# Attention and S5 output products issued in longer stretches, and a planner with new cost figures

## The chip, the cores and the metric

The kernel runs on one core of one Trainium2 chip. The metric is the device time of one execution in microseconds (us); several executions are timed and their median counts. One more execution is recorded by the hardware profiler, and all rows below are from it.

## The reference, cut to what matters

Two layers of a causal decoder trunk over 1024 tokens of width 1024, float32. Each layer is a mixer and a convolutional FFN, each followed by a residual and a LayerNorm. The mixer has an attention branch (6 heads of 64), an RG-LRU branch and an S5 state-space branch. The two places that the change touches are these products:

```python
out = jnp.einsum('bnchqk,bnkchd->bnqchd', probs, vb)          # attention: probabilities times values
...
y = (jnp.einsum('bsgp,gcp->bsgc', x_re, c_re.astype(f32))     # S5: outputs from the states,
     - jnp.einsum('bsgp,gcp->bsgc', x_im, c_im.astype(f32))   # and from the inputs within a block
     + d.astype(f32) * uf)
```

The kernel computes attention over the three dilations as one masked softmax, and S5 over blocks of 8 tokens: an output is a product of a table TK with the block's own inputs plus a product of a table CA with the states before the block.

## The kernel before

The dense projections and the FFN run as three float32r products each (high times high, high times low, low times high), 128x128 by 128x512. The FFN uses a seven-product scheme (tiles `uP` up, `dP` down). Attention's transposes and its products with the values, and all of S5, are plain float32; each such matmul shows as two matmul records in the trace.

Nothing is issued where the code states it. Engine calls are first only noted down (`Traced`), as a list of (function, arguments). `Graph` works out from tiles and regions which call needs which, and `estimate` gives each call a time; `HANDOVER` gives the delay until another engine sees a result. `sweep` and `improve` are a list scheduler that goes backward and forward over this graph with the numbers of buffers as limits (8 PSUM banks, 46 slots of 128x1024, 8 half slots of 128x512), and `make_plan` repeats it with the order that the framework makes of it (five cycles) and keeps the plan that its own model finds shortest. `issue` then issues the calls in the plan's order. All instructions therefore carry one line, L149, and are told apart by tile names.

Attention (`attend`) goes by pairs of heads p (3 per layer). For each pair there are four steps Q of 256 query rows with n = 2Q+2 key blocks of 128. `score` makes the scores (`s`), the softmax on VectorE and ScalarE (`P`). `apply(Q)` then, for each key block j, transposes the probabilities of both heads on TensorE into a bank (`pt`), copies them to a half slot (`PT`, on VectorE and ScalarE by turns), and multiplies with the values (`pv`): one matmul per head, both over 128 key rows, the first head into output partitions 0 to 63 of the bank `o`, the second into 64 to 127. So each uses one half of the array's columns. The product for block j is noted right after the copy for block j+1, and each matmul is a call of its own for the planner. In the last block of each Q only 128 query columns are computed. `fill` puts dense projections of the next pair of heads between.

S5's `outputs` makes, for each half h of the 8 group pairs, four group pairs q and two row blocks b: one TK matmul (128 rows by 128 columns, over 128 inputs) and two CA matmuls (a = real, imaginary; each over the 64 states in partitions b*64 to b*64+63, so one half of the array's rows). All go to one bank per b (`yps`). S5's `states` makes products into `vps` with column halves by turns.

The planner's figures before, for the operations concerned:

```python
HANDOVER = {"PE": 230, "DVE": 90, "ACT": 120, "POOL": 100, "SP": 0}
...
VECTOR = {"tensor_tensor": (145, 1.044), "scalar_tensor_tensor": (205, 1.05), "tensor_scalar": (180, 0.53),
```

Of the kernel before, what the change touches and what calls it, by code (L numbers as in the profile page):

```python
# [9 lines left out]
F32 = mybir.dt.float32  # L10
# [30 lines left out]
RESP = 1  # L41
HOOKS = ((0, 1, "outputs_in"), (0, 7, "glu"))
# [75 lines left out]

class NoSlot(Exception):
# [3 lines left out]
class Planner:  # L123
# [21 lines left out]
    def issue(self, tc):  # L145
        last = {}
        for n in self.order:
            f, args, kwargs = self.calls[n]
            i = f(*args, **kwargs)  # L149
            i = getattr(i, "ins", i)  # L150
            self.position[i.name] = n
            if f.__name__ == "matmul":
                bank = args[0].tensor.name
                if kwargs.get("start") and bank in last:
                    tc.add_manual_dep(i, last[bank], mybir.DependencyInfo(mybir.DependencyClass.NoSync,
                                                                          mybir.DependencyReason.DATA),
                                      reason="a bank's groups one after the other")
                last[bank] = i.name

    def scheduled(self, tc):  # L160
        return [self.position[i.name] for block in tc.compile_state.ordered_instructions_by_block.values()
                for i in block if i.name in self.position]

    def place(self, order):
        use = {}
        for t, c in enumerate(order):
            _, args, kwargs = self.calls[c]
            for a in (*args, *kwargs.values()):
                n = self.tile_of(a)
                if n is not None:  # L170
                    use[n] = (use.get(n, (t,))[0], t)
        plan, held = {}, {}
        for n, (first, last) in sorted(use.items(), key=lambda x: x[1]):
# [8 lines left out]

BANK_ALL = (1 << 4096) - 1
ENGINES = {"PE": "PE", "DVE": "DVE", "Activation": "ACT", "Pool": "POOL", "SP": "SP"}
HANDOVER = {"PE": 230, "DVE": 90, "ACT": 120, "POOL": 100, "SP": 0}
DMA_BYTES, DMA_DELAY = 380, 2000
VECTOR = {"tensor_tensor": (145, 1.044), "scalar_tensor_tensor": (205, 1.05), "tensor_scalar": (180, 0.53),
          "tensor_tensor_scan": (130, 2.1), "tensor_tensor_reduce": (250, 0.85)}
# [6 lines left out]
class Graph:  # L195
# [7 lines left out]
    def __init__(self, planner):  # L203
# [7 lines left out]
        for c, (f, args, kwargs) in enumerate(calls):  # L211
            self.engine.append(ENGINES[str(f.__self__.engine).split(".")[-1]])
# [61 lines left out]
    def estimate(self, c, name, outs, ins):  # L274
        e = self.engine[c]
        n = size(outs[0].ap[1:])
        if e == "PE":
            if name == "transpose":
                t = n / 1.2 + 2
            elif ins[0].dtype == F32R:  # L280
                t = (n + 34) / 2.4
            elif outs[0].shape[0] == 64 and n > 127:
                t = n * 1.55 / 2.4
            else:
                t = (2 * n + 8) / 2.4
        elif e == "SP":
            t, self.bytes[c] = 60, size(outs[0].ap) * 4
        else:
            n = max([n] + [size(a.ap[1:]) for a in ins])
            if e == "ACT":  # L290
                t = 205 + 0.83 * n + (150 if n == 1024 and outs[0].dtype == F32 else 0)
            elif e == "POOL":
                t = 200 + n
            elif name == "scalar_tensor_tensor" and len(outs[0].ap) > 2 and n == 1024:
                t = 2125
            else:
                a, b = VECTOR.get(name, (145, 1.044))
                t = a + b * n
        self.time[c] = round(t)
# [137 lines left out]
class Traced:  # L437
# [5 lines left out]
    def __getattr__(self, name):  # L443
        f = getattr(self.engine, name)
        return lambda *args, **kwargs: self.calls.append((f, args, kwargs))

# [53 lines left out]
def emit(tc, A, out, planner, trace):  # L500
    nc = tc.nc
    V, ACT, POOL, PE, SP = (Traced(e, planner.calls) for e in (nc.vector, nc.scalar, nc.gpsimd, nc.tensor, nc.sync))
    with ExitStack() as ctx:
# [397 lines left out]
        class S5:  # L901
# [29 lines left out]
            def states(self):  # L931
# [3 lines left out]
                for h in range(2):  # L935
                    hv = slice(h * 512, h * 512 + 512)
                    vps = [bank(f"vps{l}{a}{h}") for a in range(2)]
                    for a in range(2):
                        for q in range(4):
                            gp = h * 4 + q  # L940
                            for g2 in range(2):
                                PE.matmul(vps[a][g2 * 64:(g2 + 1) * 64, q * 128:(q + 1) * 128],
                                          lhsT=T["WvT"][a][:, gp * 128 + g2 * 64:gp * 128 + g2 * 64 + 64],
                                          rhs=U[g2][:, gp * 128:gp * 128 + 128], start=True, stop=True)
# [15 lines left out]
            def outputs(self):  # L960
# [3 lines left out]
                for h in range(2):  # L964
                    yps = [bank(f"yps{l}{b}{h}") for b in range(2)]
                    for q in range(4):
                        gp = h * 4 + q
                        c, d = slice(gp * 128, gp * 128 + 128), slice(q * 128, q * 128 + 128)
                        for b in range(2):
                            PE.matmul(yps[b][:, d], lhsT=T["TK"][b][:, c], rhs=U[b][:, c], start=True, stop=False)  # L970
                        for a in range(2):
                            for b in range(2):
                                p = slice(b * 64, b * 64 + 64)
                                PE.matmul(yps[b][:, d][:, 1:], lhsT=T["CA"][a][p, c], rhs=self.x[a][p, c][:, :127],
                                          start=False, stop=a == 1)
# [188 lines left out]
        def attend(l, p, qq, kk, vt, fill, hooks):  # L1164
# [29 lines left out]
            def apply(Q):  # L1194
                o = bank(f"o{l}{p}{Q}")
                n = 2 * Q + 2
                prev = None

                def pv(j, PT):
                    lo = 1 if j == n - 1 else 0  # L1200
                    for h in range(2):
                        PE.matmul(o[h * 64:h * 64 + 64, lo * 128:256],
                                  lhsT=vt[:, j * 128 + h * 64:j * 128 + h * 64 + 64],
                                  rhs=PT[:, h * 256 + lo * 128:h * 256 + 256], start=j == 0, stop=j == n - 1)

                for j in range(n):
# [12 lines left out]
                    if prev:  # L1219
                        pv(*prev)  # L1220
                    prev = (j, PT)
                    yield
                pv(*prev)
# [594 lines left out]
```

## Time and profile before

| what | value |
| --- | --- |
| executions timed | 2301.6, 2303.13 and 5909.03 us; median 2303.13 us |
| profiled execution, its own time | 2303.53 us |
| its span, first to last instruction | 2301.7 us |
| TensorE (PE) busy | 2242.8 us, 97% |
| weight loads (PEld) busy | 1811.4 us, 79% |
| VectorE (DVE) busy | 2045.1 us, 89% |
| ScalarE (ACT) busy | 1154.0 us, 50% |

An engine counts as busy while an instruction of its own runs; instructions overlap at their ends, so the distance from start to start tells what one costs in a dense row, and the duration tells when its result is there. In the timeline, equal instructions in a row are merged: "x4" is four records.

### The profile page before, as it was taken

Reading aid. Unit: us, or ns where it says so; the run is one execution under the profiler, and the core shown is the slowest. Engines: PE = TensorE matmul, PEld = TensorE weight load, DVE = VectorE, ACT = ScalarE, POOL = GpSimd, SP = SyncE. Lnnn points to the kernel's source line nnn. Section 1 sums busy time; section 2 is a strip of 40 time slices with the busy share of each in tenths; the row PEclk is TensorE's granted clock in tenths of the full one; section 3 lists DMA queues with packets and bytes.
Section 4 is the critical chain, followed back from the end, with each engine's and each line's share of the span. In section 5 each row is a group of like instructions: output and inputs, shape, how many; then the busy total and the mean of one; then the engine's idle time right before and its main releaser. Section 6 shows DMA issues by size and latency. Waiting matters only on the chain.

```text
span 2301.7 us, 28256 instructions
## 1 busy us (share of the span) xinstructions
PE 2242.8 (97%) x10520; PEld 1811.4 (79%) x10520; DVE 2045.1 (89%) x3357; ACT 1154.0 (50%) x1773; POOL 4.0 (0%) x8
## 2 busy tenths in 40 slices
PE   8999999999999999999998899999999999999996
PEld 6867778878888888888886677788888888788884
DVE  8888878898888989999995877888899899899999
ACT  4275673754444445444735457727455444454441
POOL 0000000000000000000000000000000000000000
PEclk9999999999999999999999899999999999999998
DMA  5321150222233435322333521401222244363312
GB/s 208 87 80 44 33 174 29 83 83 83 92 110 138 158 108 201 110 99 103 128 101 94 180 74 42 147 36 75 91 84 99 92 155 156 108 215 111 120 69 83
DMA packets 82169, 246.38 MB, mean 107 GB/s; under 512 B 12464, under 2 KB 20784, under 8 KB 82032
## 3 DMA queue, kind: packets, MB, share of 16 engines
q1 hardware_dynamic: 82032, 244.59, 31.4%
q8 instruction: 82, 1.34, 0.2%
q14 instruction: 55, 0.45, 0.1%
HBM read 176.26 MB, written 60.82 MB: 103 GB/s over the span
## 4 chain that ended last, share of the span: by engine, by line
PE 84%; DVE 10%; ACT 3%; DMA 2%; issue 1%; DVEq 0%; ACTq 0%; SPq 0%
PE uP_n L149 34%; PE dP_n L149 17%; PE o_n L149 3%; PE s_n L149 2%; PE pt_n L149 2%; DVE yf_n L149 1%; PE yps_n L149 1%; DVE cg_n L149 1%; DMA wu_n<-in_w_up_dram 1%; DVE daP_n L149 1%; PE ups00c_n L149 1%; DVE dbP_n L149 1%; PE gtps01c_n L149 1%; PE vps_01c_n L149 1%; DVE cv_n L149 1%
## 5 line engine op out<-in xcount | busy, mean ns | idle before, releaser
L149 PE MATMUL dP_n<-dbP_n,daP_n 128*128 128x512 f32 x2016 | 462.2, 391 | 12.6 <-DVE yf_n L149 11.8
L149 PEld LDWEIGHTS dP_n<-dbP_n,daP_n 128*128 128x128 f32 x2016 | 379.6, 189 | 92.5 <-issue 12.5
L149 ACT ACTIVATE dbP_n<-wr_n 128x512 fp32r<-128x512 f32 x168 | 102.8, 627 | 104.7 <-DVE wr_n L149 49.7
L149 ACT ACTIVATE wA_n<-wu_n 128x512 fp32r<-128x512 f32 x144 | 89.9, 628 | 122.4 <-PE uP_n L149 41.9
L149 ACT ACTIVATE wS_n<-wu_n 128x512 fp32r<-128x512 f32 x144 | 90.2, 630 | 111.5 <-DVE wu_n L149 41.3
L149 ACT ACTIVATE daP_n<-gr_n 128x512 fp32r<-128x512 f32 x144 | 89.5, 628 | 112.8 <-PE dP_n L149 48.2
L149 DVE SCALAR_TENSOR_TENSOR cg_n<-ga_n,small,cg_n 128x1023 f32<-128x1023 f32 x96 | 122.9, 1280 | 23.4 <-ACT cg_n L149 22.6
L149 DVE SCALAR_TENSOR_TENSOR cv_n<-va_n,small,cv_n 128x1023 f32<-128x1023 f32 x96 | 122.8, 1280 | 16.2 <-ACT cv_n L149 16.0
L149 DVE TENSOR_TENSOR yf_n<-yf_n,dP_n 128x512 f32<-128x512 f32 x192 | 127.9, 689 | 4.4 <-PE dP_n L149 2.4
L149 DVE TENSOR_TENSOR dbP_n<-wr_n,dbP_n 128x512 fp32r<-128x512 f32 x168 | 116.0, 694 | 0.3 <-ACT dbP_n L149 0.3
L149 DVE TENSOR_TENSOR daP_n<-gr_n,daP_n 128x512 fp32r<-128x512 f32 x144 | 99.8, 694 | 2.4 <-ACT daP_n L149 2.4
L149 DVE TENSOR_TENSOR wS_n<-wu_n,wS_n 128x512 fp32r<-128x512 f32 x144 | 98.2, 687 | 3.3 <-ACT wS_n L149 2.8
L149 DVE TENSOR_TENSOR wA_n<-wu_n,wA_n 128x512 fp32r<-128x512 f32 x144 | 97.8, 687 | 3.1 <-ACT wA_n L149 2.9
L149 ACT ACTIVATE cg_n<-ga_n,small 128x1024 f32<-128x1024 f32 x48 | 59.7, 1243 | 73.9 <-DVE ga_n L149 51.2
L149 PE MATMUL pt_n<-ident,P_n 128*128 128x128 f32 x432 | 74.3, 285 | 11.2 <-DVE P_n L149 10.1
L149 PEld LDWEIGHTS pt_n<-ident,P_n 128*128 128x128 f32 x432 | 53.4, 144 | 33.7 <-DVE P_n L149 11.6
L149 DVE CUSTOM_DVE_ANT_0 P_n<-s_n,mask_n 128x512 f32<-128x512 f32 (+3 forms) x96 | 55.4, 586 | 22.6 <-PE s_n L149 21.9
L149 ACT ACTIVATE cv_n<-va_n,small 128x1024 f32<-128x1024 f32 x48 | 59.4, 1238 | 24.7 <-DVE va_n L149 18.5
L149 PE MATMUL o_n<-PT_n,vt_n 128*64 128x256 f32 (+1 forms) x480 | 71.1, 375 | 0.0
L149 DVE TENSOR_TENSOR uu_n<-uP_n,p_n 128x512 f32<-128x512 f32 x96 | 65.9, 687 | 3.7 <-PE uP_n L149 3.4
L149 PE MATMUL uP_n<-T1T4h_n,wA_n 128*128 128x512 f32 x192 | 64.0, 394 | 2.1 <-DVE uu_n L149 2.1
L149 PE MATMUL uP_n<-T0T3h_n,wS_n 128*128 128x512 f32 x192 | 63.4, 391 | 2.3 <-DVE uu_n L149 2.3
(2279 smaller groups left out, 5974.7 us busy)
## 6 DMA issues: line engine op xcount, KB each, us to landing
wu_n<-in_w_up_dram SPq DMA_DIRECT2D x96, 512.0 KB, 3.5
gd<-cg_n SPq DMA_DIRECT2D x48, 512.0 KB, 2.9
gr_n<-gd SPq DMA_DIRECT2D x48, 512.0 KB, 4.4
wr_n<-in_w_down_dram SPq DMA_DIRECT2D x48, 512.0 KB, 5.1
yr_n<-hres SPq DMA_DIRECT2D x24, 512.0 KB, 3.8
hres<-yr_n SPq DMA_DIRECT2D x24, 512.0 KB, 3.2
hres<-y_n SPq DMA_DIRECT2D x16, 512.0 KB, 2.6
yf_n<-hres SPq DMA_DIRECT2D x16, 512.0 KB, 5.2
```

What stands on the lines that cost most here:

```text
L149: i = f(*args, **kwargs)
```

## The change

Three things. First, a list of calls can be bound into one `Row`, which the planner places as a single call and `issue` issues one after the other. The products with the values are bound in rows of the key blocks named in `RUNS`: for Q = 0 both blocks, for Q = 1 all four, for Q = 2 three and three, for Q = 3 four and four; a row is noted after the copy of its last block. S5's `states` products are bound in rows of one a and half. Second, in S5's `outputs` the TK matmuls are split in two column halves (m) and the order is changed: one row with all TK matmuls of a half h, then one row with all its CA matmuls, b changing with each. Third, the figures of `estimate` are new, with 350 ns (`TURN`) added for each row.

```diff
+RUNS = ((2,), (4,), (3, 6), (4, 8))
...
+TURN = 350
...
-HANDOVER = {"PE": 230, "DVE": 90, "ACT": 120, "POOL": 100, "SP": 0}
-DMA_BYTES, DMA_DELAY = 380, 2000
-VECTOR = {"tensor_tensor": (145, 1.044), "scalar_tensor_tensor": (205, 1.05), "tensor_scalar": (180, 0.53),
-          "tensor_tensor_scan": (130, 2.1), "tensor_tensor_reduce": (250, 0.85)}
+HANDOVER = {"PE": 215, "DVE": 125, "ACT": 150, "POOL": 100, "SP": 0}
+DMA_BYTES, DMA_DELAY = 370, 2050
+VECTOR = {"scalar_tensor_tensor": (127, 1.044), "tensor_scalar": (95, 0.55), "tensor_tensor_scan": (47, 2.1),
+          "tensor_tensor_reduce": (165, 1.0)}
+OTHER = 66, 1.044
...
             elif ins[0].dtype == F32R:
                 t = (n + 34) / 2.4
-            elif outs[0].shape[0] == 64 and n > 127:
-                t = n * 1.55 / 2.4
+            elif n == 1:
+                t = 109
             else:
-                t = (2 * n + 8) / 2.4
+                t = n * (8 if outs[0].shape[0] == ins[0].shape[0] == 128 else 4 if outs[0].shape[0] == 32 else 2) / 2.4
...
-                t = 205 + 0.83 * n + (150 if n == 1024 and outs[0].dtype == F32 else 0)
+                t = 75 + 0.87 * n + 115 * (len(outs) > 1) + 150 * (n == 1024 and outs[0].dtype == F32) + 140 * (n == 256)
...
+    @contextmanager
+    def row(self):
+        n = len(self.calls)
+        yield
+        self.calls[n:] = [(Row(self.calls[n:]), (), {})]
...
-                    for q in range(4):
-                        gp = h * 4 + q
-                        c, d = slice(gp * 128, gp * 128 + 128), slice(q * 128, q * 128 + 128)
-                        for b in range(2):
-                            PE.matmul(yps[b][:, d], lhsT=T["TK"][b][:, c], rhs=U[b][:, c], start=True, stop=False)
-                        for a in range(2):
+                    at = [(slice(q * 128, q * 128 + 128), slice((h * 4 + q) * 128, (h * 4 + q) * 128 + 128))
+                          for q in range(4)]
+                    with PE.row():
+                        for d, c in at:
                             for b in range(2):
-                                p = slice(b * 64, b * 64 + 64)
-                                PE.matmul(yps[b][:, d][:, 1:], lhsT=T["CA"][a][p, c], rhs=self.x[a][p, c][:, :127],
-                                          start=False, stop=a == 1)
+                                for m in (slice(0, 64), slice(64, 128)):
+                                    PE.matmul(yps[b][m, d], lhsT=T["TK"][b][:, c][:, m], rhs=U[b][:, c],
+                                              start=d.start == 0, stop=False, skip_group_check=True)
+                    with PE.row():
+                        for d, c in at:
+                            for a in range(2):
+                                for b in range(2):
+                                    p = slice(b * 64, b * 64 + 64)
+                                    PE.matmul(yps[b][:, d][:, 1:], lhsT=T["CA"][a][p, c], rhs=self.x[a][p, c][:, :127],
+                                              start=False, stop=a == 1, skip_group_check=True)
...
+                def pv():
+                    with PE.row():
+                        for j, PT in ready:
+                            lo = 1 if j == n - 1 else 0
+                            for h in range(2):
+                                PE.matmul(o[h * 64:h * 64 + 64, lo * 128:256],
+                                          lhsT=vt[:, j * 128 + h * 64:j * 128 + h * 64 + 64],
+                                          rhs=PT[:, h * 256 + lo * 128:h * 256 + 256], start=j == 0, stop=j == n - 1)
+                    ready.clear()
...
-                    if prev:
-                        pv(*prev)
-                    prev = (j, PT)
+                    ready.append((j, PT))
+                    if j + 1 in RUNS[Q]:
+                        pv()
                     yield
-                pv(*prev)
```

## Rows read from the trace of the kernel before

**Rows 1.** The page: busy time by engine, and the chain that ended last by engine.

```profile
PE 2242.8 (97%) x10520; PEld 1811.4 (79%) x10520; DVE 2045.1 (89%) x3357; ACT 1154.0 (50%) x1773; POOL 4.0 (0%) x8
...
PE 84%; DVE 10%; ACT 3%; DMA 2%; issue 1%; DVEq 0%; ACTq 0%; SPq 0%
```

**Rows 2.** Windows: stretch, length, busy us by engine, granted clock, DMA share, GB/s.

```profile
82.00:110.00 28.00, 28.00 (x149) 21.84 (x148) 22.09 (x25) 9.14 (x12) 0.00 (x0) 1.00 0.28 81
1197.00:1243.00 46.00, 46.00 (x226) 37.12 (x225) 18.95 (x17) 14.40 (x18) 0.00 (x0) 1.00 0.34 87
1243.00:1294.00 51.00, 37.16 (x164) 28.15 (x164) 47.12 (x99) 31.10 (x54) 0.00 (x0) 0.82 0.36 113
2025.00:2280.00 255.00, 244.08 (x1071) 201.83 (x1071) 252.14 (x408) 109.60 (x182) 0.00 (x0) 0.98 0.34 120
...
200.00:315.00 115.00, 115.00 (x635) 82.09 (x632) 92.23 (x173) 72.99 (x121) 0.00 (x0) 1.00 0.25 79
```

**Rows 3.** Timeline of PE: start us, us, instruction; one key block alone.

```profile
306.62 0.39 PE L149 MATMUL gtps01c_n<-xTh_n,wgt01l_n 128*128 128x512 f32 x1
306.94 0.65 PE L149 MATMUL o_n<-PT_n,vt_n 128*64 128x256 f32 x4
307.52 0.50 PE L149 MATMUL gtps01c_n<-xTh_n,wgt01h_n 128*128 128x512 f32 x1
307.85 0.39 PE L149 MATMUL gtps01c_n<-xTl_n,wgt01h_n 128*128 128x512 f32 x1
```

**Rows 4.** Timeline of PE: four key blocks in one stretch.

```profile
169.11 0.40 PE L149 MATMUL q02pc_n<-xTl_n,q02wh_n 128*128 128x512 f32 x1
169.44 1.95 PE L149 MATMUL o_n<-PT_n,vt_n 128*64 128x256 f32 x16
...
171.65 0.39 PE L149 MATMUL q02pc_n<-xTh_n,q02wh_n 128*128 128x512 f32 x1
```

**Rows 5.** Timeline of PE: one head of a block alone.

```profile
160.77 0.65 PE L149 MATMUL o_n<-PT_n,vt_n 128*64 128x256 f32 x2
161.35 0.33 PE L149 MATMUL pt_n<-ident,P_n 128*128 128x128 f32 x1
```

**Rows 6.** Instructions of the tiles `o` and `PT`: durations in ns, first and last start.

```profile
L149 PE MATMUL o_n<-PT_n,vt_n x480: 272/379/688, 125.5 to 1449.5; 128*64 128x256 f32 x128, 128*64 128x128 f32 x32
...
L149 ACT ACTIVATE PT_n<-pt_n x60: 361/582/606, 126.0 to 1445.9; 128x512 f32<-128x512 f32 x36, 128x256 f32<-128x256 f32 x24
```

**Rows 7.** The chain that ended last, in order of time, second layer.

```profile
1214.47 8.25 PE yps_n L149 x48
...
1230.42 8.25 PE yps_n L149 x48
...
1245.02 1.54 PE s_n L149 x10
```

**Rows 8.** Timeline of PE: column halves by turns in `states`.

```profile
1176.98 1.97 PE L149 MATMUL vps_n<-U_n,WvT_n 128*64 128x128 f32 x32
1178.88 0.66 PE L149 MATMUL vtp_n<-ident,vr_n 128*128 128x128 f32 x4
```

**Rows 9.** Timeline of PE: S5's products, row halves by turns for once.

```profile
102.53 0.37 PE L149 MATMUL yps_n<-xr_n,ca_n 64*128 64x127 f32 x1
102.54 0.37 PE L149 MATMUL yps_n<-xi_n,ca_n 64*128 64x127 f32 x1
102.74 0.27 PE L149 MATMUL yps_n<-xr_n,ca_n 64*128 64x127 f32 x1
102.76 0.48 PE L149 MATMUL yps_n<-xi_n,ca_n 64*128 64x127 f32 x3
103.17 0.49 PE L149 MATMUL yps_n<-U_n,tk_n 128*128 128x128 f32 x2
```

**Rows 10.** Timeline of VectorE in the last FFN.

```profile
2101.28 0.68 DVE L149 TENSOR_TENSOR gr_n<-gr_n,ds_n 128x512 f32<-128x512 f32 x1
2101.89 0.69 DVE L149 TENSOR_TENSOR dbP_n<-wr_n,dbP_n 128x512 fp32r<-128x512 f32 x1
```

More of the change, by code (lines that the diff above doesn't have):

```diff
@@ L2 @@
 import math
-from contextlib import ExitStack
+from contextlib import ExitStack, contextmanager
 import numpy as np
@@ L116, in layout, with __init__, parts @@
     return {k: np.ascontiguousarray(v, dtype=f) for k, v in arrays.items()}
+class Row:
+    def __init__(self, calls):
+        self.calls = calls
+def parts(call):
+    return call[0].calls if isinstance(call[0], Row) else [call]
 class NoSlot(Exception):
@@ L146, in issue @@
         last = {}
-        for n in self.order:
-            f, args, kwargs = self.calls[n]
+        for n, (f, args, kwargs) in ((n, c) for n in self.order for c in parts(self.calls[n])):
             i = f(*args, **kwargs)
@@ L160, in scheduled @@
     def scheduled(self, tc):
-        return [self.position[i.name] for block in tc.compile_state.ordered_instructions_by_block.values()
-                for i in block if i.name in self.position]
+        last = {}
+        for block in tc.compile_state.ordered_instructions_by_block.values():
+            for i in block:
+                if i.name in self.position:
+                    n = self.position[i.name]
+                    last.pop(n, None)
+                    last[n] = i
+        return list(last)
     def place(self, order):
@@ L166, in place @@
         for t, c in enumerate(order):
-            _, args, kwargs = self.calls[c]
-            for a in (*args, *kwargs.values()):
+            for a in (a for _, args, kwargs in parts(self.calls[c]) for a in (*args, *kwargs.values())):
                 n = self.tile_of(a)
@@ L210, in __init__ @@
         seen = {}
-        for c, (f, args, kwargs) in enumerate(calls):
-            self.engine.append(ENGINES[str(f.__self__.engine).split(".")[-1]])
+        for c, (f, args, kwargs) in ((c, x) for c, call in enumerate(calls) for x in parts(call)):
+            if c == len(self.engine):
+                self.engine.append(ENGINES[str(f.__self__.engine).split(".")[-1]])
+                self.time[c] = TURN * isinstance(calls[c][0], Row)
             kw = dict(kwargs)
@@ L938, in states @@
                     for a in range(2):
-                        for q in range(4):
-                            gp = h * 4 + q
[L941 to L944, printed above, removed]
+                        with PE.row():
+                            for q in range(4):
+                                gp = h * 4 + q
+                                for g2 in range(2):
+                                    PE.matmul(vps[a][g2 * 64:(g2 + 1) * 64, q * 128:(q + 1) * 128],
+                                              lhsT=T["WvT"][a][:, gp * 128 + g2 * 64:gp * 128 + g2 * 64 + 64],
+                                              rhs=U[g2][:, gp * 128:gp * 128 + 128], start=True, stop=True)
                     mul(vr[:, hv], vps[0], er[:, hv])
@@ L1196, in apply @@
                 n = 2 * Q + 2
[L1197 to L1204, printed above, removed]
+                ready = []
+                def pv():
+                    with PE.row():
+                        for j, PT in ready:
[5 more added lines that the diff above has]
+                    ready.clear()
                 for j in range(n):
```

8 lines of the change are left out of this document (3 added, 5 removed).

## The prediction, made before the change was run

> **What bounds the kernel now.** I read the page first: TensorE is busy 97% of the span and carries 84% of the chain that ended last, VectorE 10% [rows 1]. So the time is TensorE's queue, unless a stretch says otherwise. The windows say where it does [rows 2]. In both S5 stretches (82 to 110 and 1197 to 1243) TensorE is busy without a break, with VectorE at 79% and 41%. In attention of the first layer (200 to 315) TensorE is again unbroken and VectorE at 80%. Right after S5 in the second layer (1243 to 1294) it turns: VectorE is busy 47.1 of 51 us, TensorE stands idle for 13.8 us, and its granted clock falls to a mean of 0.82, which means that for a part of it TensorE ran at the lower of its two levels, 1.2 instead of 2.4 GHz. In the last FFN (2025 to 2280) both are full, VectorE with 252 of 255 us, and TensorE loses 10.9. What the change shortens thus lies in stretches where TensorE alone is the bound, and the time there should go down by what leaves its queue.
>
> The profiled execution took 2303.53 us for a span of 2301.7; the difference of 1.8 us stays. It is 0.4 us from the median of the executions, so I make the sum against 2303.5.
>
> **Products with the values.** A dense product takes one step of 0.227 us (the projections around these stretches; 306.62 shows the row). One key block alone, with a projection before and after it: from 306.62 to 307.85 are 1.23 us, in which two projections would take 0.454, so the block costs 0.78 [rows 3]. Four blocks in one stretch: from 169.11 to 171.65 are 2.54, less 0.454 makes 2.09 [rows 4]. So a further block costs (2.09 - 0.78) / 3 = 0.436, and a stretch has a fixed cost of 0.78 - 0.436 = 0.344 us, paid where TensorE goes over to half its columns and back.
>
> How often is it paid? There are 480 records [rows 6], four to a key block, 120 key blocks. I counted the stretches in TensorE's timeline: 85 without another instruction between, the first at 125.5, the last ending with the record at 1449.5. After the change there are 6 rows for each pair of heads (1 + 1 + 2 + 2), times 3 pairs and 2 layers: 36. The fixed costs fall by (85 - 36) x 0.344 = 16.9 us. Next to transposes the price is some 0.05 lower, so 14.5 is the low end.
>
> Second, 15 of the 85 are two records only, one head alone [rows 5]: 0.58 us until the next instruction, as much as the four records at 306.94 take to 307.52. The other half of the columns is empty for it. Two heads apart cost one block's 0.436 more than two heads together; 15 halves make some 7.5 blocks, 3.3 us. In a row the heads stand side by side. Together **20 us**, from 17 to 23.
>
> What is queued behind: a row can't start before its last copy `PT` is done, where `pv` before needed one copy. A copy takes 0.58 us on ScalarE [rows 6], and transposes of the block come before it. The planner may put projections there, since it still places copies and rows apart; cover is there wherever `fill` has projections. I take it as nothing; if uncovered, it is about 1 us for each row, see the rivals. A row of four holds four of the eight half slots, so two rows are just possible at once. Copies, transposes and DMAs are as many as before; no DMA is moved past another by hand.
>
> **S5's outputs.** In the second layer the chain shows each half as one piece: 48 records in 8.25 us, at 1214.47 and again at 1230.42 [rows 7]. The four halves of both layers come to 33 us (in the first layer they are cut up, with the same sum within 1). There TK (whole array) and CA (half the rows) alternate, and every change costs.
>
> After: a TK row has 16 matmuls, 32 records of 128 columns, in column halves by turns. That is the shape of the stretch in `states`: 32 records from 1176.98 to 1178.88, 1.90 us [rows 8]. A CA row has 32 records as well, with row halves by turns, and no stretch of before shows that at length. The nearest: at 102.53 two records of different halves start 0.01 apart, then two more after 0.20, 0.02 apart [rows 9]; so they do run together. Steady, a record alone costs 0.11 (the stretch from 102.76: three records, of which the last two follow at 0.11). Ends: 16 pairs x 0.11 = 1.8, or 32 single x 0.11 = 3.5. I take 2.0, for the rows at 102.53 are the operation itself. With 0.3 for changes at the edges a half then takes 1.90 + 2.0 + 0.3 = 4.2, saved 4.05, four times **16 us**; with single records 10. Neither end is below nothing: even single, the records are those of before with fewer changes. TK in column halves by itself saves nothing against a whole-array TK in a dense row, both 0.11 per 128 columns of both halves; what it buys is that the change back and forth is gone.
>
> Cover of these stretches: VectorE is busy 41% in 1197 to 1243 [rows 2], and the scores of the first pair of heads (1245.02) start 6.3 us of projections after S5's second half (1230.42 + 8.25) [rows 7]. So 8 us less S5 in the second layer bring the scores forward by as much. Rows of `states`: 8 of them where the trace shows 6 stretches; the fixed cost says 0.7 us at most, against some pieces that become whole: nothing, -1 to +1.
>
> **Estimates anew.** They change no instruction, only the order. Against the rows: VectorE's 128x512 operations follow each other at 0.61 us and last 0.68 [rows 10]; the old figure was 145 + 1.044 x 512 = 680 ns, the new one 66 + 535 = 601, with the rest in the handover (125). A block's two products were 2 x 165 = 331 ns, are now 427; measured 436. A half of S5's outputs was 24 calls of 110, 2.6 us, where the chain has 8.25; it is now two rows, 2.1 each. So the old plan thought VectorE an eighth too slow and TensorE's attention and S5 far too fast. The place where that hurts is in the rows: TensorE is filled with S5 and next projections up to 1245 while VectorE idles (41%), then VectorE is full and TensorE starves, 13.8 us idle and some time at the lower clock [rows 2]. A plan that knows the true prices would start the scores earlier and keep the filling work for later. No row prices a plan. Bounds: it may win most of that place (20 us), or, being another order altogether, lose as much elsewhere (the kernel has 59 us of idle TensorE in all, 2301.7 - 2242.8). I take 13 us won, nearer to the upper end because the misjudged place is visible.
>
> **The sum.** 2303.5 - 20 - 16 - 13 = **2254 us**, 2.1% less.
>
> **Rivals.**
> *The new order wins nothing.* VectorE's full stretches (2025 to 2280) stay, and every stretch gets new small waits. Then only the instructions' savings count: 2303.5 - 36 = 2267. For it: a plan with a better model can't remove the full VectorE. Against it: the starving place above. If the new order loses 10 us as well, 2277.
>
> *The new order wins more.* The starving places at 1243 and at the beginning of attention in the first layer both close, the clock stays up: 30 us on top of the 36, 2237.
>
> *The rows don't hold.* The framework makes its own order of what is issued, and if it puts ready projections between a row's matmuls, as they stand between the blocks now, the fixed costs come back: of 20 us about 3 stay, S5 keeps some 10: 2290. Against it: the 8.25 us pieces of S5, 48 records without anything between, and 16 records at 169.44, show that neighbours in the plan mostly stay neighbours.
>
> *Slower: rows that wait.* TensorE takes its instructions in order; a row whose last copy is late holds everything behind it, and the copy in turn waits in ScalarE's or VectorE's queue. 36 rows eat the gain of 36 us at 1 us of wait each, the price of one uncovered copy with its transposes; slower by 2% needs (46 + 36) / 36 = 2.3 us each, and gives 2350. For it: VectorE is at 80% in attention. Against it: the blocks now wait for their copies too, and TensorE is unbroken from 200 to 315.
>
> *Column halves don't overlap.* If the two halves of TK ran one after the other, a TK row would take 32 x 0.11 = 3.5 instead of 1.9, four times 1.6: 2260. The rows of `states` speak against it. The Trainium skill, "TensorE: Matmul & The Clock Gate", Part 3, says that a weight load overlaps running matmuls only when its row group differs, which column halves don't offer; by that rule this rival is the likely one. The trace disagrees: 32 records of column halves in 1.90 us, 0.06 each, where one alone takes 0.11.
>
> **How the numbers follow.** Chances: forecast 0.44, wins nothing or a little less 0.33, wins more 0.13, rows don't hold 0.05, rows that wait 0.03, halves apart 0.02. Two per cent, about what a measurement of this kernel can tell from no change, lie at 2257. The forecast's own range, 2244 to 2264, falls on both sides of it, more below: 0.36 of 0.44; with "wins more" that is 0.49 for faster. Slower by over 2% has 0.02 of the waiting rows and a little of an order gone wrong, 0.03. Within 2%: 0.48. The range for 8 in 10 leaves out the rows that wait, most of those that don't hold, and the outer ends of a new order: 2230 to 2284.
>
> **What would show it.** The value products: about 36 stretches of `o` and none of one head alone; S5's outputs: pieces of some 4.2 us for a half, CA records in pairs 0.01 apart. In 1197 to 1294 fewer idle microseconds of TensorE, the clock at 1.00, the first scores of the second layer sooner after S5's products than now. The FFN's stretches as long as now. I am wrong if TensorE's idle time in attention grows by what its work shrinks (then the softmax on VectorE is the bound), if the full VectorE of the FFN sets the end, or if the new plan moves waits into the FFN.

## The result, and the profile after

The changed kernel takes 2246.11 us (2244.16 to 2247.45, four executions) against 2303.13 us: a ratio of 0.9752, 95% interval 0.9733 to 0.9771, so 57.0 us less and faster by more than 2%. The forecast was 2254 us with 2230 to 2284. The profiled execution took 2247.45 us for a span of 2245.6. One execution of before, 5909.03 us, stands far off the others and is left out of the comparison.

The page gives the first reading, the busy time by engine:

```profile
PE 2205.3 (98%) x10584; PEld 1799.8 (80%) x10584; DVE 2042.5 (91%) x3357; ACT 1156.4 (51%) x1776; POOL 4.0 (0%) x8
```

Against [rows 1], TensorE's busy time fell from 2242.8 to 2205.3, 37.5 us of work (time at the lower clock included), and its idle time, span less busy, from 58.9 to 40.3, 18.6 us. VectorE and ScalarE have the same work. These two numbers can be had for every kernel below, and the study is read by them: work that a product costs, and idle time that the order leaves.

Where it went, by windows cut at the same events in both kernels (first score of a layer, first `uP`, last `dP`). Columns as in [rows 2]. Before:

```profile
0.00:115.00 115.00, 106.31 (x552) 86.27 (x553) 98.27 (x314) 42.89 (x59) 2.04 (x6) 1.00 0.47 147
115.00:437.00 322.00, 316.87 (x1639) 245.18 (x1638) 265.71 (x485) 195.13 (x314) 0.00 (x0) 0.99 0.24 74
437.00:1135.00 698.00, 693.48 (x3069) 570.77 (x3068) 649.59 (x953) 347.21 (x524) 1.92 (x2) 1.00 0.33 115
1135.00:1245.00 110.00, 109.48 (x591) 88.86 (x590) 80.38 (x141) 47.34 (x71) 0.00 (x0) 1.00 0.37 111
1245.00:1585.00 340.00, 324.32 (x1638) 250.24 (x1637) 283.34 (x502) 191.44 (x311) 0.00 (x0) 0.97 0.28 96
1585.00:2290.00 705.00, 691.69 (x3040) 569.91 (x3039) 659.34 (x950) 329.39 (x495) 0.00 (x0) 0.99 0.32 112
```

After:

```profile
0.00:115.00 115.00, 103.98 (x584) 84.45 (x584) 96.74 (x313) 42.45 (x59) 2.04 (x6) 0.99 0.50 160
115.00:424.00 309.00, 307.57 (x1628) 245.56 (x1628) 264.92 (x486) 200.99 (x318) 0.00 (x0) 0.99 0.22 73
424.00:1124.00 700.00, 696.36 (x3081) 571.31 (x3081) 649.46 (x947) 348.10 (x530) 1.91 (x2) 1.00 0.34 117
1124.00:1212.00 88.00, 88.00 (x568) 73.01 (x566) 83.29 (x152) 43.96 (x68) 0.00 (x0) 1.00 0.49 149
1212.00:1531.00 319.00, 317.22 (x1683) 254.52 (x1682) 279.59 (x498) 189.88 (x307) 0.00 (x0) 1.00 0.28 92
1531.00:2234.00 703.00, 691.60 (x3046) 570.81 (x3045) 660.04 (x952) 330.47 (x499) 0.00 (x0) 0.99 0.33 113
```

Both FFNs are as long as before (700 and 703 for 698 and 705). The rest lies in the mixers: 13 us from the first layer's first score to its FFN, 22 us between that FFN's last product and the second layer's first score (projections and S5), 21 us from there to the second FFN. In the stretch before the scores VectorE now has 83.3 of 88 us where it had 80.4 of 110: the scores come 22 us sooner after the FFN, and more of the matmuls now stand behind the first score (1683 for 1638). What followed them is in the windows of the starving place and of the last FFN, to be read against the third and fourth of [rows 2]:

```profile
1206.00:1257.00 51.00, 49.36 (x261) 39.43 (x260) 47.85 (x99) 34.13 (x60) 0.00 (x0) 1.00 0.43 130
1969.00:2224.00 255.00, 243.96 (x1069) 201.29 (x1069) 251.81 (x409) 108.81 (x182) 0.00 (x0) 0.98 0.34 120
```

TensorE idles for 1.6 of 51 us in place of 13.8, and the granted clock stays at 1.00 in place of 0.82. The last FFN keeps its full VectorE and its 11 us.

Part of the 37.5 us is the clock. Before, TensorE was busy for 23.9 us at the lower of its two levels, in four stretches (131.8 to 138.6, 1261.6 to 1275.3, 1288.9 to 1295.7, 2268.5 to 2282.2), two of them in the starving place:

```profile
1261.60:1275.30 13.70, 8.62 (x33) 7.24 (x34) 11.78 (x24) 7.82 (x11) 0.00 (x0) 0.50 0.43 129
1288.90:1295.70 6.80, 5.13 (x13) 3.36 (x14) 6.77 (x15) 2.86 (x5) 0.00 (x0) 0.50 0.39 140
```

After, it was 12.5 us, in three (93.1 to 96.5, 117.0 to 120.4, 2212.8 to 2226.4). At the lower level a step takes about twice as long (kernels 8 and 10 below), so, as an estimate, half of the 11.5 us of difference, 5.7 us, is what the clock gave back.

The value products, eight matmuls of the last row of a Q as one stretch, in TensorE's timeline (the answer to [rows 4]; the merged line gives the form of its first record):

```profile
227.53 0.39 PE L160 MATMUL xps00c_n<-xTh_n,wx00l_n 128*128 128x512 f32 x1
227.85 1.73 PE L160 MATMUL o_n<-PT_n,vt_n 128*64 128x256 f32 x16
229.51 0.50 PE L160 MATMUL xps00c_n<-xTh_n,wx00h_n 128*128 128x512 f32 x1
229.85 0.40 PE L160 MATMUL xps00c_n<-xTl_n,wx00h_n 128*128 128x512 f32 x1
```

From 227.53 to 229.85 are 2.32 us; less two steps of 0.227 that is 1.87 for three full blocks and a half one, where 0.344 + 3.5 x 0.436 makes 1.87. There are 41 stretches, not 36, and three of them are one head alone, where none was forecast: the framework put something between in a few rows.

S5's outputs and the first score in the second layer, timeline of TensorE:

```profile
1188.29 2.02 PE L160 MATMUL yps_n<-U_n,tk_n 128*64 128x128 f32 x32
...
1196.14 1.97 PE L160 MATMUL yps_n<-U_n,tk_n 128*64 128x128 f32 x32
1198.03 0.49 PE L160 MATMUL yps_n<-xr_n,ca_n 64*128 64x127 f32 x4
1198.36 0.39 PE L160 MATMUL yps_n<-xi_n,ca_n 64*128 64x127 f32 x4
...
1201.48 0.39 PE L160 MATMUL yps_n<-xi_n,ca_n 64*128 64x127 f32 x4
1201.80 0.50 PE L160 MATMUL q11pc_n<-ln20t0h_n,q11wh_n 128*128 128x512 f32 x1
...
1212.14 0.28 PE L160 MATMUL s_n<-k10a_n,q10a_n 128*128 128x256 f32 x1
```

A TK row takes 1.9 us; both CA rows together, 64 records, take 1198.03 to 1201.80, 3.77 us, four records in 0.22: the row halves run in pairs. Together 7.6 where [rows 7] have 16.5. The first score starts 10.3 us after S5's products, where it was some 6 before: the forecast sign that it would come sooner after them did not show. It comes sooner because S5's outputs now begin at 1188, not at 1214. In the first layer it is another picture:

```profile
88.73 0.50 PE L160 MATMUL q01pc_n<-xTl_n,q01wh_n 128*128 128x512 f32 x1
89.16 0.48 PE L160 MATMUL yps_n<-xr_n,ca_n 64*128 64x127 f32 x2
90.98 0.48 PE L160 MATMUL yps_n<-xi_n,ca_n 64*128 64x127 f32 x2 [1.33 <-DVE xi_n L160]
91.31 0.38 PE L160 MATMUL yps_n<-xr_n,ca_n 64*128 64x127 f32 x2
91.53 0.38 PE L160 MATMUL yps_n<-xi_n,ca_n 64*128 64x127 f32 x2
...
93.21 3.56 PE L160 MATMUL yps_n<-U_n,tk_n 128*64 128x128 f32 x28
96.70 0.48 PE L160 MATMUL yps_n<-xr_n,ca_n 64*128 64x127 f32 x2
```

Two records in 0.22, not four: for most of these records the framework issued one b before the other, so nothing was there to pair with (kernel 8 below holds the order and has the pairs). And the TK row at 93.21 needs 3.5 us for 28 records, where 32 take 1.9 in the second layer: it ran at the lower clock (93.1 to 96.5).

### The profile page after: what moved, and what is told of

Read it like the earlier page. It is cut to its first block, busy times and chain, and to the rows that moved or that the text cites. A ratio compares the mean times of both kernels' runs of the same rounds, so it can differ in the third digit from the quotient of the medians.

```text
span 2245.6 us, 28405 instructions
## 1 busy us (share of the span) xinstructions
PE 2205.3 (98%) x10584; PEld 1799.8 (80%) x10584; DVE 2042.5 (91%) x3357; ACT 1156.4 (51%) x1776; POOL 4.0 (0%) x8
## 4 chain that ended last, share of the span: by engine, by line
PE 57%; DVE 6%; DMA 1%; ACT 1%; issue 0%; DVEq 0%; ACTq 0%; SPq 0%
PE uP_n L160 22%; PE dP_n L160 19%; DVE yf_n L160 1%; PE s_n L160 1%; PE o_n L160 1%; PE pt_n L160 1%; DVE cg_n L160 1%; DVE cv_n L160 1%; DMA wu_n<-in_w_up_dram 1%; PE vps_12c_n L160 1%; PE gtps10c_n L160 1%; PE gtps11c_n L160 1%; PE q10pc_n L160 1%; PE vps_10c_n L160 1%; PE q12pc_n L160 0%; PE k10pc_n L160 0%
## 5 line engine op out<-in xcount | busy, mean ns | idle before, releaser
L160 DVE SCALAR_TENSOR_TENSOR cg_n<-ga_n,small,cg_n 128x1023 f32<-128x1023 f32 (+1 forms) x96 | 122.7, 1280 | 15.8 <-ACT cg_n L160 15.4
L160 DVE SCALAR_TENSOR_TENSOR cv_n<-va_n,small,cv_n 128x1023 f32<-128x1023 f32 (+1 forms) x96 | 122.6, 1280 | 5.8 <-ACT cv_n L160 5.5
L160 DVE CUSTOM_DVE_ANT_0 P_n<-s_n,mask_n 128x512 f32<-128x512 f32 (+3 forms) x96 | 55.3, 587 | 17.2 <-PE s_n L160 16.7
L160 PEld LDWEIGHTS pt_n<-ident,P_n 128*128 128x128 f32 x432 | 52.7, 140 | 19.6 <-issue 5.2
L160 PE MATMUL uP_n<-T0T4h_n,wA_n 128*128 128x512 f32 x192 | 63.8, 394 | 2.2 <-DVE uu_n L160 2.2
L160 PE MATMUL uP_n<-T0B11h_n,wA_n 128*128 128x512 f32 x192 | 64.8, 393 | 0.4 <-DVE wA_n L160 0.4
L160 PE MATMUL uP_n<-T1B11h_n,wA_n 128*128 128x512 f32 x192 | 64.7, 393 | 0.0
```

## The experiments

Times are medians in us. Work is TensorE's busy time by the page, idle is span less that, and the last two columns are the busy time of the records that write `o` and `yps` (windows over the whole span, those instructions alone).

| kernel | time | work | idle | `o` | `yps` |
| --- | --- | --- | --- | --- | --- |
| before (2302.1 to 2302.4 beside kernels 1 to 12) | 2303.1 | 2242.8 | 58.9 | 71.2 | 33.1 |
| changed | 2246.1 | 2205.3 | 40.3 | 57.8 | 20.2 |
| 1 new figures only | 2282.5 | 2240.6 | 41.0 | 75.0 | 33.0 |
| 2 old figures | 2270.6 | 2216.5 | 53.3 | 58.7 | 25.1 |
| 3 S5 as before | 2265.1 | 2217.1 | 45.6 | 57.8 | 33.0 |
| 4 value products as before | 2266.5 | 2227.7 | 37.8 | 79.1 | 15.4 |
| 5 rows by head | 2259.3 | 2221.6 | 35.6 | 79.3 | 18.8 |
| 6 CA by b | 2237.6 | 2203.4 | 32.0 | 57.4 | 22.6 |
| 7 whole TK | 2240.8 | 2198.7 | 41.1 | 56.4 | 21.7 |
| 8 rows held | 2236.1 | 2197.5 | 37.4 | 56.5 | 16.1 |
| 9 a row per block | 2268.3 | 2227.5 | 41.4 | 72.7 | 18.4 |
| 10 TURN 300 | 2253.8 | 2212.6 | 44.0 | 57.5 | 24.8 |
| 11 rows held, whole TK | 2244.4 | 2201.9 | 42.0 | 57.8 | 15.6 |
| 12 rows held, longer | 2244.6 | 2195.5 | 43.3 | 57.8 | 16.0 |

Work and idle are of the one profiled execution. It took 4.6 us more than the median in kernel 10 and 4.0 less in kernel 12; elsewhere it lies within 2.4 us of it.

The theory: three shares that add up, the value products' changes of the array's shape, S5's, and an order that knows true prices. The rivals: the order is all of it, or a lucky draw, or one of the products is hidden anyway.

**1. New figures only.** The kernel before with the constants and `estimate` of the change.

```diff
-HANDOVER = {"PE": 230, "DVE": 90, "ACT": 120, "POOL": 100, "SP": 0}
+HANDOVER = {"PE": 215, "DVE": 125, "ACT": 150, "POOL": 100, "SP": 0}
...
```

> The kernel before with the new figures of the planner alone; every product is issued as a call of its own, as before. My theory: instructions and order add up, and the order alone is worth the 23 us that the new profile leaves after 20 for the value products and 13 for S5, so about 2281 us (2268 to 2292), with the idle place of TensorE at the start of the second layer's attention mostly gone. Rival 1, the gain by order is a lucky draw of this one plan: 2295 to 2310. Rival 2, the new figures carry nearly all of it and the rows little: 2255 to 2262.

Measured: 2282.5 us, ratio 0.9916 (0.9901 to 0.9931). TensorE's work is that of before (2240.6), the idle time that of the changed kernel (41.0). The same work is made up otherwise: the value products now stand in 100 stretches, 26 of them one head alone (85 and 15 before), and only 7 us are busy at the lower clock (23.9 before). The windows of the second layer, up to the first score at 1233 and 51 us on:

```profile
1160.00:1233.00 73.00, 73.00 (x412) 58.35 (x412) 60.29 (x106) 22.51 (x30) 0.00 (x0) 1.00 0.41 112
1233.00:1284.00 51.00, 51.00 (x263) 40.65 (x262) 45.48 (x101) 34.64 (x60) 0.00 (x0) 1.00 0.27 82
```

VectorE is as full as before after the first score (45.5 of 51), but TensorE has no idle time there and the full clock. So the figures alone close the starving place, and as a whole they are worth 20 us. Which of the new figures did it was not tried.

**2. Old figures.** The changed kernel with the planner of before.

```diff
-TURN = 350
+TURN = 0
...
-HANDOVER = {"PE": 215, "DVE": 125, "ACT": 150, "POOL": 100, "SP": 0}
+HANDOVER = {"PE": 230, "DVE": 90, "ACT": 120, "POOL": 100, "SP": 0}
...
```

> The changed kernel with the planner's old figures (and no added time for a row): rows and S5's new products stay. My theory: 2303.5 - 20 - 13 = 2270 us (2260 to 2280), with TensorE idle at the start of attention as before. Rival 1 (lucky draw of one plan): any plan may come out, 2245 to 2300, and the idle places lie elsewhere. Rival 2 (figures carry it): 2295 to 2303.

Measured: 2270.6 us, 0.9863 (0.9848 to 0.9878). The rows alone are worth some 31 us, and the idle time is back at 53.3. Rows alone and figures alone make 31.5 + 19.6 = 51 of the 57.0. "All by the figures" falls. But the idle time lies only in part where it was expected, at the start of the second layer's attention (first score at 1222.63); most of the rest of what the changed kernel doesn't have is a wait in the first layer:

```profile
85.02 0.79 PE L160 MATMUL q01pc_n<-xTh_n,q01wl_n 128*128 128x512 f32 x1 [7.95 <-DVE q01wl_n L160]
...
1222.63 0.58 PE L160 MATMUL s_n<-k10a_n,q10a_n 128*128 128x256 f32 x1 [4.31 <-DVE k10a_n L160]
```

```profile
1222.00:1273.00 51.00, 47.80 (x226) 36.74 (x228) 46.00 (x99) 31.59 (x55) 0.00 (x0) 0.87 0.38 110
```

With the wait that ends at the first score some 7 us are idle there, where before had 13.8. That the idle places move was the sign of the rival "lucky draw". Against that rival speaks the table: both orders made with the old figures leave 53.3 and 58.9 us idle, all twelve made with the new ones (some with one constant changed) 32.0 to 45.6.

**3. S5 as before.** The changed kernel, with the order of `outputs` and whole-array TK of before.

```diff
-                    with PE.row():
-                        for d, c in at:
-                            for b in range(2):
-                                for m in (slice(0, 64), slice(64, 128)):
...
+                    for q in range(4):
...
+                            PE.matmul(yps[b][:, d], lhsT=T["TK"][b][:, c], rhs=U[b][:, c], start=True, stop=False)
```

> The changed kernel with S5's outputs as before (whole-array TK, q by q, no rows there). My theory: S5's stretches are back at some 33 us, so 2246 + 13 = 2259 us (2252 to 2268). Rival, S5's stretches are hidden behind waits of VectorE and cost nothing on the path: 2246 to 2249.

Measured: 2265.1 us, 19 more than the changed kernel; `yps` 12.8 busy us more, idle 5.3 more. S5's products are on the path. The share is larger than expected, by the idle time of another order.

**4. Value products as before.** The changed kernel, each matmul with the values a call of its own again.

```diff
...
-                    ready.append((j, PT))
-                    if j + 1 in RUNS[Q]:
-                        pv()
+                    if prev:
+                        pv(*prev)
+                    prev = (j, PT)
...
```

> The changed kernel with the value products as before (each a call of its own after the next block's copy). My theory: some 80 to 90 stretches of value products again, 2246 + 20 = 2266 us (2258 to 2276). Rival, the softmax on VectorE paces attention, so that the shorter products bought nothing: 2246 to 2250.

Measured: 2266.5 us, 20.4 more. VectorE doesn't pace attention. But this isn't the arrangement of before: there are 106 stretches, not 80 to 90, and 34 of them are one head alone; `o` takes 79.1 us, more than the 71.2 of before. On the other side S5's rows came out whole in both layers, and `yps` took 15.4 us, 4.8 less than in the changed kernel. The work went up by 22.4 us. 65 stretches at 0.32 us (kernel 9) and 31 heads alone at half of 0.436 make 27.6, less 4.8 is 22.8.

**5. Rows by head.** Only the order inside a value row changes.

```diff
-                        for j, PT in ready:
-                            lo = 1 if j == n - 1 else 0
-                            for h in range(2):
+                        for h in range(2):
+                            for j, PT in ready:
+                                lo = 1 if j == n - 1 else 0
```

> The changed kernel, with the matmuls inside a value row ordered by head: all blocks for the first head, then all for the second. The plan's calls, times and rows are the same, and there are as many changes to half columns and back. My theory (the two column halves run at the same time only when they alternate): a key block costs some 0.86 us in place of 0.436, over 96 full blocks and 24 half ones 42 + 5 = 47 us more TensorE time, so about 2293 us (2280 to 2300). [...]

Measured: 2259.3 us, 13 more, 43 stretches: outside the range, and clear of the 2246 at which it would have stayed if the order made no difference. `o` is busy for 21.5 us more, so alternating is worth a lot. The prediction weighed a rule of the Trainium skill ("TensorE: Matmul & The Clock Gate", Part 3), that a weight load overlaps running matmuls only when its row group differs. If that kept column halves apart, the order would make no difference; the trace disagrees. But 21.5 is half of the 47 us. The timeline shows a row of four full blocks, and one of a full block and a half one:

```profile
126.42 0.88 PE L160 MATMUL o_n<-PT_n,vt_n 128*64 128x256 f32 x8
...
224.72 2.86 PE L160 MATMUL o_n<-PT_n,vt_n 128*64 128x256 f32 x16
227.51 0.33 PE L160 MATMUL pt_n<-ident,P_n 128*128 128x128 f32 x1
```

2.79 us from 224.72 to the next instruction, where [rows 4] take 1.88 (from 169.44 to the next projection at 171.32) and 16 records one after the other at 0.216 would take 3.46. Taken one by one, the first records start 0.22 apart, then two series run side by side from 225.64 to 226.34, then records start 0.22 apart again. So the second head's matmuls begin before the first head's are all through. In the short row at 126.42 records start in pairs 0.01 apart throughout, and its 0.88 us are what the changed kernel's alternating row takes (0.87 at 129.93). So the rows didn't run purely by head. Whether the framework issued them partly alternating, as it reorders S5's rows, or TensorE itself overlaps more than neighbours, isn't shown: no run holds the order of such a row. Where records of one head stand apart they take 0.216 each, as the 0.86 us a block assumed. In the time, work of 16.3 us more meets 4.7 us less idle, from another order.

**6. CA by b.** The two row halves don't alternate.

```diff
-                        for d, c in at:
-                            for a in range(2):
-                                for b in range(2):
+                        for b in range(2):
+                            for d, c in at:
+                                for a in range(2):
```

> The changed kernel, with CA's row ordered by b, so that the row halves don't alternate; the rest is the same. My theory: records alone at 0.11 us each. In the second layer, where the new trace shows pairs, 64 records more at full price, 64 x 0.056 = 3.5 us; in the first layer the framework has already put most of them by b, and at most 1.5 us are left to lose: 2246 + 4 = 2250 us (2247 to 2254), with all CA records 0.11 apart. Rival, alternating rows are worth nothing because the two row halves wait for each other: 2246.

Measured: 2237.6 us, 8.5 less than the changed kernel where 4 more were expected. `yps` did go up, by 2.4 us: in the second layer, where the changed kernel has pairs, from 7.8 to 11.2, the 3.5 that were said, while the first layer took 1.0 less. The time fell because this order left 32.0 us idle, 8.3 less. The mechanism shows in the work and is too small for the time.

**7. Whole TK.** TK on the whole array, in the change's rows, at the same planned time.

```diff
-                                for m in (slice(0, 64), slice(64, 128)):
-                                    PE.matmul(yps[b][m, d], lhsT=T["TK"][b][:, c][:, m], rhs=U[b][:, c],
+                                PE.matmul(yps[b][:, d], lhsT=T["TK"][b][:, c], rhs=U[b][:, c],
...
```

> The changed kernel with TK on the whole array again, but in the rows of the change; the planner's time for these rows is kept the same. My theory: a whole-array matmul of 128 columns is 0.22 us in a dense row, the same as its two halves side by side, and it needs no change of the array's shape next to projections: 2246 us, 1 us less to 1 more (2241 to 2250). Rival, the change's own figure of 8 steps a column (0.427 us a matmul, twice the halves): 32 x 0.21 = 7 us more, 2253 (2251 to 2257).

Measured: 2240.8 us. `yps` 21.7, with CA again by b in the first layer, some of it at the lower clock. Not the 7 us of the rival: in the second layer, where both kernels have whole rows, `yps` is 7.9 against 7.8. Kernel 11 has this in both layers.

**8. Rows held.** In `issue`, for two neighbours of one row:

```diff
...
+            if previous[0] == n:
+                tc.add_manual_dep(i, previous[1], mybir.DependencyInfo(mybir.DependencyClass.NoSync,
+                                                                       mybir.DependencyReason.DATA),
+                                  reason="a row's products one after the other")
+            previous = n, i.name
```

> The changed kernel with the order inside a row held: each matmul of a row is put behind the one before it by an order-only dependency, which adds no semaphore. My theory: the framework's own order broke S5's rows in the first layer, where 46 of 64 CA records stand alone at 0.11 us; held rows give pairs there, some 2.5 us, and with fewer changes of shape 3 to 5 in all: 2242 us (2237 to 2247). Rival, holding the row makes TensorE wait at its head for the later table, which costs what the pairs give: 2246 to 2250.

Measured: 2236.1 us, 0.9715 (0.9702 to 0.9728), the lowest of all, though not clear of kernel 6 (0.9706 to 0.9732); work 7.8 us less than the changed kernel's, `yps` 16.1, in the first layer 8.1 for 12.4. So it was the order inside the rows that had broken the pairs (by their starts 40 of the 64 records stood alone, not 46), though a part of the 4.3 us is the clock. It isn't free of new waits, in TensorE's timeline of the first layer:

```profile
88.17 1.96 PE L161 MATMUL yps_n<-U_n,tk_n 128*64 128x128 f32 x30
96.61 0.79 PE L161 MATMUL k01pc_n<-xTh_n,k01wl_n 128*128 128x512 f32 x1 [6.49 <-DVE k01wl_n L161]
97.21 0.63 PE L161 MATMUL k01pc_n<-xTh_n,k01wh_n 128*128 128x512 f32 x1
97.63 0.63 PE L161 MATMUL k01pc_n<-xTl_n,k01wh_n 128*128 128x512 f32 x1
```

TensorE waits 6.5 us for a split weight on VectorE, and then steps at 0.43 us, the lower clock, where 0.227 is usual.

**9. A row per block.** `RUNS` names every block.

```diff
-RUNS = ((2,), (4,), (3, 6), (4, 8))
+RUNS = ((1, 2), (1, 2, 3, 4), (1, 2, 3, 4, 5, 6), (1, 2, 3, 4, 5, 6, 7, 8))
```

> The changed kernel with a row for every key block (120 rows; as issued they make 111 stretches, where the changed kernel has 41); both heads still stand side by side, no head is alone. My theory, a stretch has a fixed cost of 0.344 us for going over to half columns and back: 70 x 0.344 = 24 us more work of TensorE, so 2246 + 24 = 2270 us, less or more by what another order does (2258 to 2278). Rival, the gain of the long rows was that no head stands alone and not the changes saved: 2246 (2238 to 2252).

Measured: 2268.3 us, 22.2 more, all of it work (22.2); by 70 stretches that is 0.32 us each. The trace has 111 stretches; 7 are one head alone, where the changed kernel has 3.

**10. TURN 300.** The same instructions, another order.

```diff
-TURN = 350
+TURN = 300
```

> The changed kernel with 300 in place of 350 ns as the planner's added time for a row: the same instructions, another draw of the order. My theory: TensorE's work stays within 3 us, its idle time lies between 30 and 45 us as in the other variants, and the changed kernel with 40.3 was a rather poor draw: 2236 to 2246. Rival, the order hangs on the figures being exact, and 350 is the best: 2248 to 2256.

Measured: 2253.8 us (2251.95 to 2258.42), 7.7 more. My theory expected the other sign: the changed kernel isn't a poor draw. Idle is 44.0, within the range, but work is 7.3 us more, where at most 3 were expected, though no instruction differs. Windows and timeline say why for the larger part:

```profile
84.00:106.00 22.00, 19.91 (x120) 17.01 (x119) 20.76 (x20) 10.00 (x11) 0.00 (x0) 0.80 0.43 90
97.40:107.70 10.30, 9.61 (x46) 8.40 (x45) 8.45 (x7) 5.50 (x6) 0.00 (x0) 0.50 0.37 103
```

```profile
96.28 0.48 PE L160 MATMUL yps_n<-xi_n,ca_n 64*128 64x127 f32 x2 [1.41 <-DVE xi_n L160]
96.60 0.39 PE L160 MATMUL yps_n<-xr_n,ca_n 64*128 64x127 f32 x2
96.82 0.38 PE L160 MATMUL yps_n<-xi_n,ca_n 64*128 64x127 f32 x2
...
98.42 0.63 PE L160 MATMUL yps_n<-xr_n,ca_n 64*128 64x127 f32 x2
98.84 0.63 PE L160 MATMUL yps_n<-xi_n,ca_n 64*128 64x127 f32 x2
```

Behind a wait of 1.41 us for `xi` from VectorE, S5's first-layer records go from 0.22 to 0.43 us for two, and the granted clock is 0.50 from 97.4 to 107.7: TensorE ran at the lower level. In all it was busy there for 22.4 us in this trace, 12.5 in the changed kernel's; half of the difference, an estimate, is 4.9 of the 7.3 us. The profiled execution is also the slowest of the four. One example doesn't settle whether 350 is better for being exact; kernels 6, 7 and 8 with 350 lie 5 to 10 us below the changed one, so orders scatter by that much.

**11 and 12. Rows held with whole TK; rows held with one row of six blocks for Q = 2.** Both have kernel 8's edit; 11 adds that of kernel 7, 12 this:

```diff
-RUNS = ((2,), (4,), (3, 6), (4, 8))
+RUNS = ((2,), (4,), (6,), (4, 8))
```

> Rows held in order, and TK on the whole array. My theory: held rows bring CA to its pairs in both layers, whole-array TK costs the same as its halves; S5's stretches as short as with held rows alone, about 16 us busy, and the time 2236 us with 8 either way for the order (2228 to 2244). Rival, whole-array matmuls at twice the cost of the halves: 7 us more S5 work.

> Rows held in order, and one row of six key blocks for Q = 2 in place of two of three: 30 rows in place of 36. My theory: up to 6 x 0.344 = 2 us less work, six of eight half slots held at once: 2234 us (2226 to 2244), the order decides. Rival, six half slots held leave the copies waiting for a free one: TensorE idles in attention, 2245 or more.

Measured: 2244.4 and 2244.6 us, both just past the upper end. `yps` came as expected, 15.6 with whole TK against 16.1 with halves, so a whole-array matmul doesn't cost twice. Kernel 11 has 4.4 us more work than kernel 8 all the same, and 4.6 more idle; where the work comes from wasn't followed up. Kernel 12 has the least work of all, 2195.5, and 5.9 us more idle than kernel 8; its profiled execution took 2240.6 us, so the rest up to 2244.6 is not in the trace. It also tests less than planned: 30 rows came out as 39 stretches, one fewer than kernel 8's 40. Its idle time doesn't come from half slots that are held longer: in the first layer's attention TensorE is busy for 163.46 of 165 us.

```profile
115.00:280.00 165.00, 163.46 (x949) 128.72 (x950) 138.39 (x304) 108.99 (x192) 0.00 (x0) 1.00 0.18 53
```

## Why the prediction was right, step by step

The causes were right and all three show; the sizes of the three terms were not, and their errors partly cancel.

**Value products, 20 us.** Right in cause, some 3 us too large. 85 stretches became 41, not 36, and 15 heads alone became 3, not none. At kernel 9's 0.32 us a stretch (0.344 was worked out of [rows 3, 4]) and half of 0.436 for a head alone that is 44 x 0.32 + 12 x 0.218 = 16.7 us, an estimate, just under the stated 17 to 23. That kernel 4 loses 20.4 us looks like 20 by chance: it breaks up more than before had broken up, and its S5 rows give 4.8 back.

**S5, 16 us.** The mechanism was right, and where rows stayed whole so was the size: 16.5 became 7.6 us in the second layer, 8.9 where 8 was said. In the first layer the framework's order took the pairs apart and part of it ran at the lower clock, so `yps` fell from 16.2 to 12.4 there and by 12.9 in all. The rival "the rows don't hold" was half true there; kernel 8 shows it, with `yps` at 16.1. That the pairs at 102.53 [rows 9] would go on in a long row is borne out.

**Halves of TK.** That they buy nothing against a whole-array TK in a row was said, and kernel 11 shows it.

**Estimates anew, 13 us.** The term that was mis-sized. Idle time fell by 18.6 us and the clock gave back an estimated 5.7, some 24 us, above the stated bound of 20; the changed kernel against kernel 2 gives 24.5, kernel 1 alone 19.6. The forecast was for one place, and there it holds: from the second layer's first score to its FFN idle time fell from 15.7 to 1.8 us. That is 13.9 of the 18.6; the rest lay elsewhere. For this term the rival "the new order wins more", with 30 us, came nearer.

**The sum.** 16.7 for the value products, 12.9 for S5's records and 24.3 for order and clock make 53.9 of the 57.0 us. The rest wasn't taken apart; about 1.7 us of the clock's loss stand within S5's term. The sum missed by 8 us only, because an order term 11 too small met two others 3 too large each. That is partly luck.

**The rivals.** That the new order wins nothing falls by kernel 1, and the FFNs kept their length. Rows that wait fall too: the list of TensorE's waits in the changed kernel names no row of `o`, and its idle time from the first score to the FFN fell in both layers.

**What was not foreseen** is how far equal instructions scatter: kernel 10 and the changed kernel differ by 7.7 us for one constant, two thirds of the added work by the clock. In this kernel a forecast of a new order is hardly better than some 8 us either way. The version to keep is kernel 8, with the reserve that kernel 6 measures the same, and that its lead over the changed kernel is 7.8 us of work, which its diff explains in part, and 2.9 us of idle time, which another draw may take away.

## What to carry to other kernels

Count how often TensorE goes over to half its array and back; here each time costs some 0.32 us, so matmuls that use halves belong side by side, with the halves alternating and the order held. If a planner makes the order, check its prices against start-to-start steps of the trace: new figures as a whole won 20 us of 2300 here, where the old ones had taken VectorE for 13% too slow and S5's products for three times too fast. And judge a variant by its work and its idle time apart, since a re-planned order alone moves the time by as much as a small edit does.

## What the runs showed of the hardware

Float32 matmuls on the two column halves run side by side when they alternate: 32 records of 128 columns in 1.9 us, 0.06 each, where one alone takes 0.11. A row coded by head took 2.79 us for 16 records of 256 columns, between 1.88 for alternating ones and the 3.46 of one after the other; what made it overlap in part is open (kernel 5). Two row halves pair as well: with them alternating the second layer's `yps` is 7.8 us, without 11.2 (kernel 6). A float32 matmul on the whole array costs the same per 128 columns as its two column halves side by side (S5 busy 15.6 against 16.1 us). And the granted clock fell to the lower of its two levels soon behind a single wait of 1.41 us (kernel 10: 0.50 from 97.4 to 107.7), which doubled the step of S5's records there; what decides the fall was not tried.
